# Streamed matmul operands moved by 192 bytes relative to the weight tiles

## Chip, cores and metric

One core of a Trainium2 chip. The metric is the device time of one execution in microseconds; the time before is the median of three runs.

## What is computed

A decoder trunk of four layers on 256 tokens of width 1024, in float32. Each layer adds half a feed-forward block, a mixer, and half a second feed-forward block; a norm ends it. The mixers are gated DeltaNet (layers 0 and 3), stick-breaking attention (layer 1) and a sparse attention with latent keys (layer 2).

```python
for i in range(DEPTH):
    x = x + 0.5 * swiglu(rmsnorm(x, ffn1_norm[i]), ffn1_w_gu[i], ffn1_w_down[i])
    h = rmsnorm(x, mix_norm[i])
    x = x + mixer[i % 3](h)
    x = x + 0.5 * swiglu(rmsnorm(x, ffn2_norm[i]), ffn2_w_gu[i], ffn2_w_down[i])
return rmsnorm(x, final_norm)

def swiglu(h, w_gu, w_down):        # hidden width 2816
    gate, up = jnp.split(h @ w_gu, 2, axis=-1)
    return (jax.nn.silu(gate) * up) @ w_down
```

## The kernel before

All activations lie transposed in SBUF, features on the 128 partitions and tokens along the free axis. A float32 operand of a large product is split into a high part, rounded to the four-byte type float32r, and a low part, the rest; a product is then hi x hi, hi x lo and lo x hi summed in PSUM. All products of this kind run through line 43, `Bank.mm(out, lhsT, rhs)`: `lhsT`, a tile of 128 x 128, is loaded as the stationary operand, and `rhs` is streamed.

Weights arrive in chunks of 1 MB (`chunk`, line 164, three buffers r). A chunk is four pieces of 512 columns; `piece` writes each one's high part h on ScalarE (line 170) and its low part l on VectorE (line 171). h and l have ten buffers each. One stationary operand is 128 columns (512 bytes of each partition) of a piece, so its offset in h or l is a multiple of 512 bytes.

The streamed operands:

- x2, the layer's input times the norm's gain, split: for each of 8 tiles of features 256 columns of the high part and then 256 of the low part (lines 222 and 223). In the profile its name is x, since the program leaves out numbers.
- ah and al, the split hidden activations of the feed-forward block (lines 199 and 200).
- oh and ol, the split heads of a mixer, and lath and latl, the split latents of the sparse attention.

A feed-forward block has 11 steps of 256 hidden columns. A step's gate and up projections (`tile_wide`) are 64 products into bankG: in turn a wide one, h with 512 columns of x2 (high and low part side by side), and a narrow one, l with 256 columns of the high part. Its down projection (`rows`) is 48 products into bankA, each of 256 columns of ah or al. There are 8 blocks, so 2,816 wide and as many narrow products of x2. In the mixers the projections are narrow products of x2 (`tiles2`), and the output projection (`out_proj`) calls `rows` with oh and ol, into bankG. In stick-breaking attention 96 products for the values have h or l as the streamed operand, 512 columns, and x2 as the stationary one. Each mixer has small products besides, in float32 and float16, into bankA.

The order of the products is fixed when the program is made: mixers' side work are generators that `pump` advances between groups of products by a count of estimated time, which no address enters.

Tiles lie in pools, one behind the other in the order const, raw, hi, lo, big, wk; each starts on a multiple of 32 bytes. Sizes and first bytes below are those of the placed program, in bytes of a partition.

| tile | pool | buffers x size | first byte | within 512 |
|---|---|---|---|---|
| h | hi | 10 x 2048 | 57184 | 352 |
| l | lo | 10 x 2048 | 77664 | 352 |
| x2 | big | 1 x 16384 | 98144 | 352 |
| oh, ol, lath, latl and others | big | 8 x 8192 | 114528 | 352 |
| ah | wk | 6 x 1024 | 194592 | 32 |
| al | wk | 6 x 1024 | 200736 | 32 |
| ntri (a table of stick-breaking) | wk | 512 | 211968 | 0 |

The distance of a product is here the first byte of the streamed operand minus that of the weight tile, within 512. It is 0 for x2, oh, ol, lath and latl with h and l (128, 256 or 384 for the products of lath and latl whose weight tiles have 96 columns), and 32 - 352, which is 192, for ah and al. Plain float32 products of two tiles of big, as kT with kT, have distance 0, and u (32) with E (big) has 192. The streamed operand of ntri starts at 320. The last tile of wk ends at byte 228808 of 229376.

Of the kernel before, what the change touches and what calls it, by code (L numbers as in the profile page):

```python
# [11 lines left out]
F32 = mybir.dt.float32  # L12
# [8 lines left out]
P = 128  # L21
T = 256          # tokens
D = 1024
KT = D // P      # k tiles of the model width
F = 2816
NS = F // 256    # steps of a feed-forward block, 256 hidden columns each
# [3 lines left out]
RS = 1024.0      # scale of the residuals kept in float16  # L30

# Everything is kept transposed: [feature on partitions, token].  A float32 matmul operand x is split
# exactly into hi = x rounded to float32r and lo = x - hi; hi*hi + lo*hi + hi*lo in PSUM carries float32.


class Bank:
    """One PSUM bank that several accumulation groups share."""
# [16 lines left out]
    def tr(self, out, x):  # L54
        """Transposes a [128, 128] float32 tile; the only kind of write to its part of the bank."""
        self.nc.tensor.transpose(out, x, self.k.ident)  # L56
        self.k.now += 0.11
# [8 lines left out]
class Trunk:  # L66

    def __init__(self, tc, ctx, a):
        self.tc, self.nc, self.a = tc, tc.nc, a
        nc = self.nc  # L70
        pool = lambda **k: ctx.enter_context(tc.tile_pool(**k))
        self.const = pool(name="const", bufs=1)
        self.raw = pool(name="raw", bufs=3)
        self.hip = pool(name="hi", bufs=10)
        self.lop = pool(name="lo", bufs=10)
        self.big = pool(name="big", bufs=8)
        self.wk = pool(name="wk", bufs=2)
        self.ps = pool(name="ps", bufs=4, space=bass.MemoryType.PSUM)
        self.side, self.now = [], 0.0
        self.act_set("silu_and_others")  # L80
        c = self.const
        self.x = c.tile([P, KT, T], F32, name="x")
        self.gains = c.tile([P, 13, KT], F32, name="gains")
        self.ones = c.tile([P, P], F32, name="ones")
        nc.gpsimd.memset(self.ones, 1.0)
        self.ident = c.tile([P, P], F32, name="ident")
        bf = c.tile([P, 2, P], BF16, name="bf")
        self.identb, self.scap = (bf[:, i] for i in range(2))
        hf = c.tile([P, 3, P], F16, name="hf")
        self.identh, self.identk, self.m1 = (hf[:, i] for i in range(3))  # L90
        self.consts = ((self.ident, a["ident"]), (bf, a["bf"]), (hf, a["hf"]))
        self.pad = c.tile([P, T], F32, name="pad")
        nc.gpsimd.memset(self.pad, 0.0)
        self.pcs = [c.tile([P, 2, 3 + T], F32, name="pc%d" % i) for i in range(2)]
        for pc in self.pcs:
            nc.gpsimd.memset(pc[:, :, :3], 0.0)

    def table(self, name):
        """A mixer's constants, side by side."""
        t = self.wk.tile([P, 1024], F32, name="tab", tag="tab", bufs=1)  # L100
        src = self.a[name]
        self.nc.sync.dma_start(t[:, :src.shape[1]], src)
        return t
# [13 lines left out]
    def bank(self, tag="A"):  # L117
        """A: small products and a feed-forward's sums; G: the big projections."""
        return Bank(self, self.ps.tile([P, 512], F32, name="bank" + tag, tag=tag))

    # ---- interleaving: side work (generators) advances between groups of the big products.  A generator
    # yields how long (us on TensorE's clock, as counted here) its next stage's operands are expected to take,
    # or a condition that its next stage waits for.
# [6 lines left out]
    def pump(self, n=None):  # L130
        """Run up to n ready stages; only the first few (width) generators are under way."""
        for _ in range(n or self.burst):
            g = min(self.side[:self.width], key=self.due, default=None)
            if g is None or self.due(g) > self.now:
                return
            self.step(g)
# [8 lines left out]
    def wait(self, done):  # L145
        """Run side work until done()."""
        while not done():
            g = min(self.side[:self.width], key=self.due)
            assert self.due(g) < math.inf
            self.now = max(self.now, self.due(g))  # L150
            self.step(g)
# [8 lines left out]
    def chunk(self, src, w=2048, pw=512, pool=(), parts=1):  # L160
        """A [128, w] chunk of weights as (hi, lo) pieces of pw columns; the pieces in pool are split by GpSimd."""
# [12 lines left out]
    def first_chunk(self, src, n):  # L174
        """The kernel's start: the first chunk and x arrive in parts and are split as they come."""
# [27 lines left out]
    def rsqrt(self, a, n):  # L203
        """Newton's iteration for a ** -0.5 on a small tile."""
# [20 lines left out]
    def norm_in(self, n):  # L225
        """x times the gain, split; the tokens' factors come later (rstd)."""
# [5 lines left out]
    def spread(self, cols):  # L232
        """[token, 1] columns (SBUF) -> a bank with each as a row on all partitions."""
# [5 lines left out]
    def rstd(self, st):  # L239
        """1 / rms(x) per token, into st: compact [token, 2] and as rows [128, T]."""  # L240
# [28 lines left out]
    # GDN's chunks of the input projection, (kind, head pair): keys 0, values 1, queries 2, gate 3  # L269
    gdn_order = ((0, 0), (0, 1), (0, 2), (3, 0), (0, 3), (3, 1), (2, 0), (1, 0), (1, 1), (1, 2), (1, 3),  # L270
                 (2, 1), (3, 2), (2, 2), (2, 3), (3, 3))
    korder = (0, 2, 4, 6, 1, 3, 5, 7)    # the order in which a block's last products finish x

    def tiles2(self, pieces, xg, order=None):
        """Two M tiles (8 k tiles each) of one chunk into one bank."""
# [8 lines left out]
    def tile_wide(self, pieces, m, order=None):  # L284
        """One M tile into a bank: the columns of hi * hi and those of hi * lo + lo * hi side by side."""
# [9 lines left out]
    def rows(self, acc, pieces, a2, last, done=None):  # L295
        """acc[d, t] += w[f, d] a[f, t] for the chunk's two k tiles."""
# [73 lines left out]
    def gdn(self, i, n):  # L370
# [17 lines left out]
        # b and a: [16, T]  # L388
# [4 lines left out]
        # pairs (head, chunk of tokens) are kept in the order of the projections: head pair, chunk, head of the pair  # L393
# [13 lines left out]
        def gates():  # L407
# [29 lines left out]
            # E[j, i] = exp(G_i - G_j) for i >= j, else 0; eGb: exp(G_i) of the second chunk as rows  # L437
# [13 lines left out]
        def conv2(b, kind, c, dst):  # L451
            """Convolution and silu of two projected heads: dst [128, 2, T]."""
# [3 lines left out]
            # chunks are stored k, v, q; the convolution's channels q, k, v  # L456
# [18 lines left out]
        def keys(c):  # L475
# [23 lines left out]
            # A = I + L (unit lower triangular), transposed, in two float16 parts  # L499
# [8 lines left out]
            # the inverse X of A in float16 by merging blocks; XT its transpose  # L508
# [26 lines left out]
            # float32: with R = I - A X, the inverse is X + X R + X R R (+ X R^3, below float32)  # L535
# [46 lines left out]
        def delta(c):  # L582
# [36 lines left out]
            # the queries' factor s = dk^-0.5 / |q| goes into the output's norm: s * rsqrt(s^2 ss/128 + eps)  # L619
# [53 lines left out]
    def sb(self, n):  # L673
# [31 lines left out]
        def attend(h, qk):  # L705
            # z^T: [keys, queries]; columns: key tile 0 x all queries, key tile 1 x queries of tile 1
# [38 lines left out]
    def rms_factor(self, sq, n, ones, out):  # L745
        """rsqrt(mean of squares + eps) per token from a squared tile, into out [token, 2]."""
# [11 lines left out]
    def dsa(self, n):  # L758
# [15 lines left out]
        # tiles of the input projection: cq 0..2, index key | rotary key 3, ckv 4..5; 6: the normed index key  # L774
# [25 lines left out]
        def weights():  # L800
            """A query's weights of the index heads, times the factor of its latent, which relu lets through."""
# [6 lines left out]
        def latents(c, b):  # L808
            """Evacuate a chunk of the input projection: factor of the token, squares, gain and split."""
# [21 lines left out]
        def index_keys():  # L831
            """kidx[:, e]: the rotated index key in the rows of a tile's head e, zeros in the other's; rotary keys into K."""
# [49 lines left out]
        def select():  # L882
            """The 64 largest of each row are struck out; what is struck out and causal is selected: neg 0, else -1e30."""
# [33 lines left out]
        def attend(h):  # L917
# [21 lines left out]
            for i in range(3):       # (key 0, query 0), (key 0, query 1), (key 1, query 1)  # L939
                bt.tr(bt.t[:, i * P:(i + 1) * P], p[:, i * P:(i + 1) * P])  # L940
# [25 lines left out]
        # the index first, so that the selection runs beside the projections of queries, keys and values  # L966
# [61 lines left out]
    def final(self, out):  # L1028
        """The last norm, beside the last products: to be called with each tile of x as it is done."""
# [53 lines left out]
def cols(w):  # L1083
    """[1024, n * 256] -> [n, 128, 2048]: per chunk two M tiles of 8 k tiles."""
# [4 lines left out]
def rows(w):  # L1089
    """[n * 256, 1024] -> [n, 128, 2048]: per chunk two k tiles."""  # L1090
# [4 lines left out]
def pack_ffn(gu, down):  # L1095
    out = np.empty((gu.shape[0], NS, 3, 128, 2048), gu.dtype)
    for l in range(gu.shape[0]):
        # a chunk: gate tile, up tile
# [6 lines left out]
def feat(g):  # L1105
    """[n * 128] -> [128, n]"""
# [3 lines left out]
def pack(x, ffn1_norm, ffn1_w_gu, ffn1_w_down, mix_norm, ffn2_norm, ffn2_w_gu, ffn2_w_down,  # L1110
# [41 lines left out]
    # constants of the shapes  # L1152
# [10 lines left out]
    for v, s in enumerate((2, 4, 8, 16, 32, 64)):  # L1163
        c = np.arange(64)
        blk = c // s                      # block of 2s of the c-th first-half column
# [41 lines left out]
```

## Time and profile before

| | us |
|---|---|
| median of three runs | 2090.61 |
| lowest and highest | 2089.94, 2092.35 |
| span of the profiled execution | 2092.3 |

The profile gives the profiled execution no time besides its span. Engines in it: PE is TensorE's products, PEld its weight loads, DVE VectorE, ACT ScalarE, POOL GpSimd, SP the queue that issues DMAs. Products are pipelined, and the end of one is modelled, so records of following products overlap, and the pitch from one start to the next is shorter than a record. In the names of a product, as bankG<-x,h, the streamed operand stands ahead of the stationary one.

### The profile page before, as it was taken

To read this page: it belongs to the slowest core of one execution; us is meant where nothing else is said; L and a number is where in the kernel's file an instruction comes from. 1 tells how busy PE (TensorE), PEld (TensorE's weight loads), DVE (VectorE), ACT (ScalarE), POOL (GpSimd) and SP (SyncE) were. 2 spreads that over 40 slices of the span, in tenths; PEclk is the share of its full clock that TensorE was granted. 3 is DMA by queue.
4 is the path that set the end of the run, shared out by engine and by line. 5 is a ranking of instruction groups with operands and counts; after the bars stand their busy time and mean duration, and the time that the engine had idled before them with its cause. 6 is when DMAs were issued, how large, how long until landed. Compare 5 with 4: busy or idle time off the path is not lost.

```text
span 2092.3 us, 38898 instructions
## 1 busy us (share of the span) xinstructions
PE 2037.1 (97%) x14762; PEld 1886.2 (90%) x14762; DVE 1646.0 (79%) x3456; ACT 1308.2 (63%) x2804; POOL 161.9 (8%) x145
## 2 busy tenths in 40 slices
PE   8999899999999999999999998999999998999998
PEld 7999899999999989999989997899989998999997
DVE  7778898877887776777787789877787788988776
ACT  6566776665665566655665664765665667766654
POOL 1001311100100010100010013100010013111000
PEclk9999999999999999999999999999999999999999
DMA  7555333555455554555555542455555553235552
GB/s 256 195 188 182 102 105 123 173 190 187 171 206 188 195 179 140 176 184 197 185 184 199 182 153 76 162 187 196 184 182 199 184 179 106 100 119 182 182 199 84
DMA packets 52603, 353.62 MB, mean 169 GB/s; under 512 B 6976, under 2 KB 7872, under 8 KB 10688
## 3 DMA queue, kind: packets, MB, share of 16 engines
q1 hardware_dynamic: 52128, 350.49, 48.4%
q8 instruction: 116, 1.90, 0.4%
q14 instruction: 71, 0.58, 0.1%
q10 hardware_dynamic: 288, 0.66, 0.1%
HBM read 350.07 MB, written 1.05 MB: 168 GB/s over the span
## 4 chain that ended last, share of the span: by engine, by line
PE 82%; DVE 12%; ACT 4%; issue 1%; POOL 0%; DMA 0%; SPq 0%; ACTq 0%; DVEq 0%; POOLq 0%
PE bankG L43 55%; PE bankA L43 25%; DVE l L171 5%; ACT x L222 1%; DVE kT L466 1%; PE bankA L56 1%; ACT h L170 1%; DVE x L223 1%; DVE rs_t L211 1%; DVE x L302 0%; DVE rs_y L212 0%; DVE rs_t L210 0%; ACT sq L244 0%; DVE vT L466 0%; DVE pc L455 0%
## 5 line engine op out<-in xcount | busy, mean ns | idle before, releaser
L43 PE MATMUL bankG<-x,h 128*128 128x512 f32 (+1 forms) x4192 | 1269.0, 361 | 12.0 <-DVE x L223 12.0
L171 DVE TENSOR_TENSOR l<-r,h 128x512 fp32r<-128x512 f32 x1328 | 936.7, 713 | 374.1 <-ACT h L170 370.9
L170 ACT ACTIVATE h<-r 128x512 fp32r<-128x512 f32 x1328 | 823.0, 627 | 595.5 <-PE bankG L43 337.4
L43 PE MATMUL bankG<-x,l 128*128 128x256 f32 x3504 | 989.2, 282 | 0.0
L43 PEld LDWEIGHTS bankG<-x,h 128*128 128x128 f32 x4192 | 751.3, 189 | 130.1 <-DVE x L223 14.9
L43 PEld LDWEIGHTS bankG<-x,l 128*128 128x128 f32 x3504 | 666.5, 190 | 0.1
L43 PE MATMUL bankA<-ah,l 128*128 128x256 f32 x1408 | 389.2, 276 | 0.0
L43 PE MATMUL bankA<-ah,h 128*128 128x256 f32 x1408 | 389.2, 276 | 0.0
L43 PE MATMUL bankA<-al,h 128*128 128x256 f32 x1408 | 389.1, 276 | 0.0
L43 PEld LDWEIGHTS bankA<-ah,h 128*128 128x128 f32 x1408 | 264.4, 188 | 3.3
L43 PEld LDWEIGHTS bankA<-al,h 128*128 128x128 f32 x1408 | 264.5, 188 | 0.0
L43 PEld LDWEIGHTS bankA<-ah,l 128*128 128x128 f32 x1408 | 264.4, 188 | 0.0
L330 DVE TENSOR_TENSOR e<-e,bankG 128x256 f32<-128x256 f32 x352 | 145.9, 414 | 4.6 <-ACT e L329 4.6
L329 ACT ACTIVATE e<-bankG 128x256 f32<-128x256 f32 x352 | 129.3, 367 | 11.5 <-PE bankG L43 11.5
L245 POOL TENSOR_TENSOR sq<-sq 128x512 f32<-128x512 f32 x12 | 15.5, 1294 | 1473.8 <-ACT sq L244 1473.8
L342 DVE TENSOR_TENSOR e<-e,rb 128x512 f32<-128x512 f32 x176 | 121.0, 691 | 5.3 <-ACT rb L259 0.2
L199 ACT ACTIVATE ah<-e 128x256 fp32r<-128x256 f32 x176 | 72.6, 417 | 21.4 <-DVE e L344 21.3
L343 ACT ACTIVATE e<-e 128x256 f32<-128x256 f32 x176 | 71.3, 405 | 7.2 <-DVE e L342 7.2
L43 PE MATMUL bankG<-oh,h 128*128 128x256 f32 x256 | 74.5, 291 | 0.0
L344 DVE TENSOR_TENSOR e<-e 128x256 f32<-128x256 f32 x176 | 73.8, 419 | 0.7 <-ACT e L343 0.7
L200 DVE TENSOR_TENSOR al<-e,ah 128x256 fp32r<-128x256 f32 x176 | 73.1, 419 | 0.5 <-ACT ah L199 0.5
L43 PE MATMUL bankG<-oh,l 128*128 128x256 f32 x256 | 72.5, 283 | 0.0
(290 smaller groups left out, 1704.7 us busy)
## 6 DMA issues: line engine op xcount, KB each, us to landing
r<-in_ffn SPq DMA_DIRECT2D x262, 1024.0 KB, 4.9
r<-in_gdn_in SPq DMA_DIRECT2D x32, 1024.0 KB, 4.9
r<-in_gdn_out SPq DMA_DIRECT2D x8, 1024.0 KB, 4.9
r<-in_sb_qk SPq DMA_DIRECT2D x8, 1024.0 KB, 4.9
r<-in_sb_v SPq DMA_DIRECT2D x4, 1024.0 KB, 4.9
r<-in_sb_out SPq DMA_DIRECT2D x4, 1024.0 KB, 4.9
r<-in_dsa_out SPq DMA_DIRECT2D x4, 1024.0 KB, 4.9
r<-in_dsa_in SPq DMA_DIRECT2D x3, 1024.0 KB, 4.8
```

The costliest lines, as they stand in the source:

```text
L43: self.nc.tensor.matmul(out, lhsT, rhs, start=self.fresh, stop=stop, skip_group_check=True)
L56: self.nc.tensor.transpose(out, x, self.k.ident)
L170: self.nc.scalar.activation(h[:, :pw], src, AF.Copy)
L171: (self.nc.gpsimd if pool else self.nc.vector).tensor_sub(l[:, :pw], src, h[:, :pw].bitcast(F32))
L199: self.nc.scalar.activation(dh, src, AF.Copy)
L200: self.nc.vector.tensor_sub(dl, src, dh.bitcast(F32))
L211: nc.vector.scalar_tensor_tensor(t, t, -0.5, a, op0=ALU.mult, op1=ALU.mult)
L329: nc.scalar.activation(e[:, m * T:(m + 1) * T], b.t[:, :T], AF.Copy)
L330: nc.vector.tensor_add(e[:, m * T:(m + 1) * T], e[:, m * T:(m + 1) * T], b.t[:, T:])
L342: nc.vector.tensor_mul(e2, e2, st["rb"][:, None, :].to_broadcast([P, 2, T]))
L343: nc.scalar.activation(e[:, :T], e[:, :T], AF.Silu)
L344: nc.vector.tensor_mul(e[:, T:], e[:, T:], e[:, :T])
```

## The change

Two tiles that nothing writes or reads are put around the pool big: one of 48 float32 numbers (192 bytes) ahead of it, one of 80 (320 bytes) behind it. All tiles of big so start 192 bytes later, and all of wk 512 bytes later; const, raw, hi and lo stay. The distance of x2, oh, ol, lath and latl to h and l becomes 192, that of h to x2 in the values of stick-breaking attention 320, and that of ah and al stays 192. Everywhere else the diff only empties comments and docstrings; lines from 77 on have numbers higher by 3.

```diff
         self.raw = pool(name="raw", bufs=3)
         self.hip = pool(name="hi", bufs=10)
         self.lop = pool(name="lo", bufs=10)
+
+        pool(name="gap0", bufs=1).tile([P, 48], F32, name="gap0")
         self.big = pool(name="big", bufs=8)
+        pool(name="gap1", bufs=1).tile([P, 80], F32, name="gap1")
         self.wk = pool(name="wk", bufs=2)
         self.ps = pool(name="ps", bufs=4, space=bass.MemoryType.PSUM)
```

## Rows read from the trace of the kernel before

**Rows 1.** The page: span, busy time of each engine, granted clock by slices

```profile
span 2092.3 us, 38898 instructions
...
PE 2037.1 (97%) x14762; PEld 1886.2 (90%) x14762; DVE 1646.0 (79%) x3456; ACT 1308.2 (63%) x2804; POOL 161.9 (8%) x145
...
PEclk9999999999999999999999999999999999999999
```

**Rows 2.** Stages: stretch, length, busy time (count) of each engine, clock, DMA

```profile
192.80:378.40 185.60, 175.22 (x1670) 169.76 (x1669) 165.97 (x440) 127.18 (x325) 40.43 (x36) 0.98 0.34 117
378.40:562.60 184.20, 183.68 (x1240) 168.31 (x1240) 142.94 (x271) 113.88 (x234) 5.34 (x4) 1.00 0.55 188
...
747.10:858.60 111.50, 109.33 (x785) 103.42 (x784) 71.28 (x141) 71.59 (x133) 5.30 (x4) 0.98 0.46 159
...
1227.60:1339.90 112.30, 101.20 (x724) 91.37 (x723) 95.37 (x269) 66.11 (x149) 29.10 (x25) 0.98 0.32 111
```

**Rows 3.** The chain of waits in a feed-forward block: start, length, what

```profile
41.43 11.10 PE bankG L43 x64
52.53 5.45 PE bankA L43 x48
```

**Rows 4.** TensorE by form, whole run: count, busy us, mean ns, idle

```profile
L43 PE MATMUL bankG<-x,h 128*128 128x512 f32 x2816 | 990.2, 394 | 11.7 <-DVE x L223 11.7
L43 PE MATMUL bankG<-x,l 128*128 128x256 f32 x3504 | 989.2, 282 | 0.0
L43 PE MATMUL bankA<-ah,l 128*128 128x256 f32 x1408 | 389.2, 276 | 0.0
...
L43 PE MATMUL bankA<-al,h 128*128 128x256 f32 x1408 | 389.1, 276 | 0.0
L43 PE MATMUL bankG<-x,h 128*128 128x256 f32 x1376 | 278.9, 292 | 0.2 <-DVE x L223 0.2
...
L43 PE MATMUL bankG<-oh,l 128*128 128x256 f32 x256 | 72.5, 283 | 0.0
L43 PE MATMUL bankG<-ol,h 128*128 128x256 f32 x256 | 72.3, 283 | 0.0
...
L43 PE MATMUL bankG<-lath,l 128*128 128x256 f32 x36 | 10.1, 282 | 0.0
...
L43 PE MATMUL bankA<-u,E 128*128 128x128 f32 x64 | 9.4, 275 | 0.0
...
L43 PE MATMUL bankA<-kT 128*128 128x128 f32 x64 | 8.4, 275 | 0.0
...
L43 PE MATMUL bankG<-lath,l 128*96 128x256 f32 x16 | 5.2, 326 | 0.0
...
L56 PE MATMUL bankA<-ident,on 128*128 128x128 f32 x32 | 4.8, 272 | 0.0
```

**Rows 5.** TensorE by form between 41.4 and 180 us, in the first block

```profile
L43 PE MATMUL bankG<-x,h 128*128 128x512 f32 x275 | 95.8, 391 | 0.0
L43 PE MATMUL bankG<-x,l 128*128 128x256 f32 x274 | 76.7, 280 | 0.0
```

**Rows 6.** The chain in the four mixers: shares by line, and two pieces

```profile
by line: PE bankG L43 32.3%; PE bankA L43 15.9%; DVE l L171 11.8%; DVE kT L466 5.3%; issue 4.1%; PE bankA L56 3.6%; DVE vT L466 1.8%; DVE rs_t L211 1.8%; DVE pc L455 1.7%; DVE qT L466 1.6%; DVE rs_t L210 1.3%; ACT x L222 1.2%; ACT h L170 1.
...
by line: PE bankG L43 70.8%; PE bankA L43 17.2%; DVE l L171 6.7%; issue 1.4%; ACT h L170 1.0%; DVE x L302 0.9%; PE bankA L56 0.6%; DVE rs_y L212 0.5%; DVE rs_t L211 0.4%; DVE rs_t L210 0.3%; DVE rs_y L208 0.1%; DVE ms L254 0.1%; ACTq L170 0
...
802.05 4.31 PE bankG L43 x36
...
by line: PE bankG L43 21.0%; DVE l L171 10.2%; PE bankA L43 8.0%; issue 6.7%; DVE m L893 4.5%; DVE m L876 4.2%; DVE m L891 3.8%; DVE rs_t L211 2.9%; ACT p L932 2.5%; DVE qtmp L910 2.4%; DVE rs_y L212 2.2%; DVE K L997 2.2%; ACT K L998 2.0%; 
...
1325.86 14.15 PE bankG L43 x118
...
by line: PE bankG L43 32.2%; PE bankA L43 15.8%; DVE l L171 11.8%; DVE kT L466 5.3%; issue 4.2%; PE bankA L56 3.3%; DVE vT L466 1.8%; DVE rs_t L211 1.8%; DVE pc L455 1.7%; DVE qT L466 1.6%; DVE rs_t L210 1.3%; ACT x L222 1.2%; ACT h L170 1.
```

**Rows 7.** Timeline of TensorE, values of stick-breaking: first and last of twelve

```profile
768.46 0.39 PE L43 MATMUL bankG<-l,x 128*128 128x512 f32 x1
768.69 0.62 PE L43 MATMUL bankG<-h,x 128*128 128x512 f32 x2
...
775.94 0.39 PE L43 MATMUL bankG<-l,x 128*128 128x512 f32 x1
```

**Rows 8.** Weight loads by form, whole run

```profile
L43 PEld LDWEIGHTS bankA<-ah,l 128*128 128x128 f32 x1408 | 264.4, 188 | 0.0
...
L43 PEld LDWEIGHTS bankG<-oh,l 128*128 128x128 f32 x256 | 49.1, 192 | 0.1
```

**Rows 9.** TensorE's waits, longest in total: us, times, longest

```profile
PE bankA L56 <- DVE rs_y L212: 12.0, 11, 2.2
PE bankG L43 <- DVE x L223: 12.0, 10, 7.5
```

**Rows 10.** VectorE by form in a feed-forward block, 395.9 to 554.7 us

```profile
L171 DVE TENSOR_TENSOR l<-r,h 128x512 fp32r<-128x512 f32 x117 | 80.7, 692 | 38.9 <-ACT h L170 38.7
```

**Rows 11.** TensorE by form in stick-breaking attention: products with ntri

```profile
L43 PE MATMUL bankA<-sl,ntri 128*128 128x384 f32 x8 | 2.7, 340 | 0.0
```

**Rows 12.** Timeline of TensorE, x2 with weights of 16 columns

```profile
197.03 0.39 PE L43 MATMUL bankA<-x,bah 128*16 128x256 f32 x2
...
198.05 0.40 PE L43 MATMUL bankA<-x,bah 128*16 128x256 f32 x2
```

## The prediction

> **What bounds the kernel now.** I read the page first, then the stages, then the chain of waits, then the groups by form. The page has TensorE busy 97% of a span of 2092.3 us, with the granted clock at 0.9 or more in every slice [rows 1]; but a busy TensorE is not a TensorE at its peak, so the stages come next. They are of two kinds. Between the marks 378.4 and 562.6 one feed-forward block takes 184.2 us, with VectorE busy 142.9, ScalarE 113.9 and the clock full; the mixers take 185.6 (gated DeltaNet), 111.5 (stick-breaking) and 112.3 (sparse attention) [rows 2]. In the chain, a step of a feed-forward block is two pieces and nothing else: 64 products into bankG in 11.10 us, then 48 into bankA in 5.45 [rows 3]. Eleven times 16.55 is 182.1 of the 184.2 us. What matters in these blocks is therefore the pitch of the products, the time from one start to the next: 11.10 / 32 = 346.9 ns for a wide and a narrow one together (512 and 256 columns), and 5.45 / 48 = 113.5 ns for each of the narrow ones of the down projection. The groups by form give longer means (276 ns for ah and al) [rows 4], since a record runs to the end of its pipeline: 276 - 113.5 = 162.5, and (391 + 280 - 346.9) / 2 = 162 for the pair [rows 5, 3]. Means less 162.5 are pitches.
>
> **The excess.** At 2.4 GHz 256 columns last 106.7 ns and 512 last 213.3. What each product takes beyond that sorts by the distance of its operands (start of the streamed operand minus start of the weight tile, within 512 bytes):
> - distance 0, narrow, in a mixer: 36 in 4.31 us, 118 in 14.15 [rows 6], so 119.7 and 119.9; excess 13.1.
> - distance 0, wide with h as the moving operand: 33 between the starts 768.46 and 775.94 [rows 7], so 226.7; excess 13.4.
> - distance 0, a wide and a narrow one in turn: 346.9 against 320; excess 26.9 for two, 13.4 each.
> - distance 192 (ah and al): 113.5; excess 6.9.
>
> So at distance 0 every product of split operands pays about 13.4 ns whatever its width, and at 192 one of 256 columns pays 6.9. The cleanest pair is oh against ah: the same function, the same shapes, the same weight tiles, 283 ns against 276 [rows 4]. The weight loads differ too, 192 ns against 188 [rows 8].
>
> **The change, part by part.** It removes and adds no instruction, no wait and no DMA; the two tiles are never written. Order, queues and buffer counts stay. (1) gap0 moves everything in big by 192 bytes. Weight and streamed operand go from distance 0 to 192 for x2, oh, ol, lath and latl, which is the distance of ah and al now. (2) gap1 makes the shift of wk 512 in all, so ah and al keep their distance.
>
> Feed-forward blocks: a pair becomes 320 + 2 x 6.9 = 333.8 ns, the 64 products 10.68 us where they took 11.10. With 8 blocks of 11 steps, 88 x 0.42 = 36.9 us. All of it reaches the end if nothing else is late: VectorE has 142.9 us of work for a block that would take 179.6, ScalarE 113.9, and the waits of TensorE are short, the longest group 12.0 us in the whole run [rows 2, 9]. Were a split late instead, VectorE's weight split would be it, 692 ns each [rows 10]; its load would be 80% of the block, so I add nothing.
>
> Mixers: a narrow product goes from 119.9 to 113.5, 5.3% of its time. Only those on the chain count. bankG holds 32.3% of 185.7 us, 32.2% of 185.6, 70.8% of 111.6 and 21.0% of 112.4 [rows 6]: 60.0 + 59.8 + 79.0 + 23.6 = 222.4 us. Of that, 96 wide ones with h moving (21.8 us) have their distance turned the other way, to 320, which no row of a product with a full weight load shows; from below, they could stay at 226.7, from above pay the 17.8 ns of excess (340 - 162.5 - 160) of the product of 384 columns with ntri, whose distance is 320 [rows 11], 96 x 4.4 = 0.4 us more. I take the same 6.4 ns as for the rest, since 320 is 192 the other way: 0.6 us. The other 200.6 us give 10.7. Bounds: none of the gain where VectorE and ScalarE work is late too (3.6 us, stick-breaking alone), and all 2,988 narrow products times 6.4 (19.1 us; 1,376 and 688 of x, 768 of oh and ol, 156 of lath and latl [rows 4]). I take 11.3, by the chain's share.
>
> Other operands that change their distance: plain float32 products. kT with kT is at 0 and u with E at 192, and both last 275 ns [rows 4]; I count nothing, with 0.3 us either way (some 100 small products, and 3 ns between 275 and the 272 of a transpose).
>
> Sum: 2092.3 - 36.9 - 11.3 = 2044.1 in the profile's terms. The profiled execution's span is 1.7 us above the median of 2090.61, so 2042.4.
>
> **A rule against it.** The Trainium skill's page SBUF — State Buffer, section Who interferes with whom, gives TensorE two independent read ports, one for the moving operand and one for weight loads, and says that it never waits on anyone. By that rule no distance could matter and the time would stay at 2090.6. The rows at 13.4 and 6.9 ns above speak against it as far as one trace can; the rule's outcome is the rival of no change below.
>
> **Rivals.**
> - *The excess at distance 192 grows with width.* 6.9 ns per 256 columns, so 13.8 for a wide product. For it: with one width only at distance 192, the trace can't tell a charge per product from one per column, and the wide rows at 226.7 are twice 113.4. Against: then the wide ones with h moving pay nothing for distance 0, while narrow ones pay 6.4. A pair would take 320 + 20.7 = 340.7, saving 6.2 x 2,816 = 17.5 us; with 10.7 from the mixers, 2092.3 - 28.2 - 1.7 = 2062.4.
> - *Only narrow products gain.* In the stretch of rows 5 the pair splits into 391 - 280 = 111 ns more for the wide one, so 229 and 118. If the 229 stays, a pair takes 342.5, saving 4.4 x 2,816 = 12.4 us, and with 10.7 from the mixers it is 2067.5.
> - *No change.* All narrow products at 120 write to bankG, all at 113.5 to bankA, so the cause could be the bank or the stage. For it: the float32 products above, both in bankA, don't care for the distance. Against: with 16-column weights, x2 at its present place streams at 0.113 (nine products between 197.03 and 198.05 [rows 12]), so x2 alone isn't slow; what is slow is x2 with a full weight load, and oh and ah differ in little but place. Also here: the placement drops the unused tiles. 2090.6.
> - *Slower.* 192 may be good only inside runs of equal products, as in the down projection, and the alternation of 512 and 256 columns may fall each time on the weight load's reads. The nearest row is the 17.8 ns of the product of 384 columns [rows 11]. Place: the gate and up projections. A pair would take 320 + 35.6 = 355.6, 8.7 x 2,816 = 24.5 us more; if narrow ones in the mixers paid it too, 222.4 x 3.8% = 8.5 more: 2123.6. With the mixers' gain kept, it decides from a pair of 350.9 ns on (346.9 + 11.3 / 2.816), or 11.23 us for the 64.
>
> **How the numbers follow.** The likeliest, every product at 6.9 ns: 0.53; its own range is 2034 (all mixer gains) to 2050 (the least). Per-column excess 0.20, narrow ones alone 0.08, still faster than 2034 0.04, no change 0.08, slower 0.07. The range 2034 to 2070 takes in the first three. I call a difference under 0.2% (4 us) the same, about what a measurement of this kernel can tell: faster 0.85, same 0.08, slower 0.07.
>
> **What would show it.** Right: in the chain 10.68 us for the 64 products (10.90 by the per-column rival, 10.96 where only narrow ones gain, 11.10 with no change, over 11.23 if slower), and 5.45 still for the 48. Means by form: 276 for x with l and for oh and ol, 383 for the wide one in a stretch like that of rows 5 (390 by the per-column rival). Mixers: 36 products of x in 4.09 us. Weight loads at 188 for oh. Blocks at 179.6 us, with VectorE's work as before; if a block is longer than its products, VectorE has become late. Wrong first of all would be the step that extends 6.9 ns from 256 columns to 512.

## The result: slower, and the profile after

The changed kernel takes 2115.41 us (median of four runs, 2113.41 to 2116.32) against 2090.36: a ratio of 1.0117, interval 1.0103 to 1.0132. The forecast was 2042.4 with a range from 2034 to 2070. The span is 2114.0 us, 21.7 more than before, with the same 38898 instructions.

The stages tell where it came from. These are the stretches of [rows 2], by the changed kernel's own marks, with the second gated DeltaNet mixer as well (stretch, length, busy time and count of each engine, clock, DMA):

```profile
194.00:377.80 183.80, 171.58 (x1671) 166.13 (x1670) 165.41 (x440) 126.68 (x325) 40.66 (x36) 0.98 0.34 117
377.80:565.90 188.10, 187.56 (x1240) 170.68 (x1239) 143.02 (x271) 113.98 (x234) 5.34 (x4) 1.00 0.53 185
754.00:863.10 109.10, 107.07 (x786) 100.86 (x786) 71.17 (x141) 71.24 (x133) 5.29 (x4) 0.98 0.46 162
1239.40:1351.10 111.70, 100.05 (x724) 90.02 (x723) 95.06 (x270) 65.91 (x149) 27.15 (x25) 0.98 0.32 111
1727.50:1911.50 184.00, 173.35 (x1670) 167.96 (x1669) 165.51 (x440) 126.62 (x324) 41.27 (x36) 0.97 0.34 115
```

The mixers became shorter: 183.8 + 109.1 + 111.7 + 184.0 = 588.6 us, where they had 185.6 + 111.5 + 112.3 + 185.6 = 595.0, so 6.4 less. A feed-forward block became longer, 188.1 where it had 184.2, and the eight of them together 21.7 + 6.4 = 28.1 us. Clock and VectorE's work in the block are as they were. The chain of waits in such a block, which answers to [rows 3], has both pieces longer:

```profile
38.89 11.31 PE bankG L43 x64
50.20 5.65 PE bankA L43 x48
```

A wide and a narrow product now take 11.31 / 32 = 353.4 ns, where 346.9 were measured and 333.8 forecast. And the products of ah and al, whose distance of 192 did not change, take 5.65 / 48 = 117.7 ns where they took 113.5. That is 88 x 0.21 and 88 x 0.20 us, 36 in all; the blocks lost less, 28.1. In part this is since a few of the steps of before already took 5.65 and 11.29 us (below), and in part luck: the 64 products that open the first block took 14.11 us in the profile before and 11.77 here, and in the runs below with the same 64 products it lies anywhere between 11.8 and 13.8.

In the mixers the forecast pitch is there, though not everywhere. The last group of the output projection in the first of them, by form, with 276 where oh and ol had 283 [rows 4], and one piece of the chain in stick-breaking attention, which had 4.31 us in [rows 6] and was forecast at 4.09:

```profile
L43 PE MATMUL bankG<-oh,l 128*128 128x256 f32 x18 | 5.0, 276 | 0.0
```

```profile
808.35 4.10 PE bankG L43 x36
```

Over the whole run, though, the changed kernel has 281 for the three kinds of ah and al, 399 for the wide products of x2 (276 and 394 in [rows 4]), and 279 for oh with l, between the two values:

```profile
L43 PE MATMUL bankG<-x,h 128*128 128x512 f32 x2816 | 1003.0, 399 | 11.6 <-DVE x L226 11.6
...
L43 PE MATMUL bankA<-ah,l 128*128 128x256 f32 x1408 | 395.6, 281 | 0.0
...
L43 PE MATMUL bankG<-oh,l 128*128 128x256 f32 x256 | 71.2, 279 | 0.0
```

So there are two questions: why do wide and narrow products in turn not gain at 192, and why did ah and al, which stayed at 192, become slower?

### The profile page after: what moved, and what is told of

Its sections match the earlier page's. It is cut to its first block, busy times and chain, and to the rows that moved or that the text cites. A ratio compares the mean times of both kernels' runs of the same rounds, so it can differ in the third digit from the quotient of the medians.

```text
span 2114.0 us, 38898 instructions
## 1 busy us (share of the span) xinstructions
PE 2056.7 (97%) x14762; PEld 1894.1 (90%) x14762; DVE 1646.3 (78%) x3456; ACT 1306.7 (62%) x2804; POOL 161.1 (8%) x145
## 4 chain that ended last, share of the span: by engine, by line
PE 84%; DVE 10%; ACT 3%; issue 1%; POOL 0%; DMA 0%; SPq 0%; DVEq 0%; ACTq 0%; POOLq 0%
PE bankG L43 56%; PE bankA L43 27%; DVE l L174 4%; ACT x L225 1%; DVE kT L469 1%; PE bankA L56 1%; DVE x L226 1%; ACT h L173 1%; DVE rs_t L214 0%; DVE rs_y L215 0%; DVE rs_t L213 0%; DVE vT L469 0%; DVE pc L458 0%; DVE qT L469 0%; ACT sq L247 0%
## 5 line engine op out<-in xcount | busy, mean ns | idle before, releaser
L43 PE MATMUL bankG<-x,h 128*128 128x512 f32 (+1 forms) x4192 | 1275.6, 363 | 11.8 <-DVE x L226 11.8
L43 PE MATMUL bankA<-al,h 128*128 128x256 f32 x1408 | 395.7, 281 | 0.0
L43 PE MATMUL bankA<-ah,l 128*128 128x256 f32 x1408 | 395.6, 281 | 0.0
L43 PE MATMUL bankA<-ah,h 128*128 128x256 f32 x1408 | 395.6, 281 | 0.0
L43 PEld LDWEIGHTS bankA<-ah,h 128*128 128x128 f32 x1408 | 270.0, 192 | 3.7
```

What stands on the lines that cost most here:

```text
L43: self.nc.tensor.matmul(out, lhsT, rhs, start=self.fresh, stop=stop, skip_group_check=True)
```

## The experiments

Each run is one edit of the kernel before or of the changed one. For runs without an interval the time is a single one; the kernel before took 2090 to 2092 us beside them. "64" and "48" are the chain's pieces of a feed-forward step.

**Is it where ah lies?** Only wk is moved, by 512 bytes.

```diff
         self.big = pool(name="big", bufs=8)
+        pool(name="gap1", bufs=1).tile([P, 128], F32, name="gap1")
```

> Only wk moves, by 512 bytes; x2, oh and ol stay at distance 0, ah and al at 192. Theory A (the pitch of ah depends on the state in which the gate and up products leave TensorE, not on where ah lies): nothing changes, 48 products of ah in 5.45 us, 64 of x2 in 11.10, span 2092 us. Theory B (512 bytes are not the period, so ah lies worse after the move of wk): 48 products of ah in 5.65 us, 64 of x2 still in 11.10, span 2092 + 88 x 0.20 = 2110 us.

Measured: 2091.0 us, and the chain is that of before.

```profile
55.86 11.10 PE bankG L43 x64
66.96 5.45 PE bankA L43 x48
```

Theory B falls: the new place of wk costs nothing.

**Does ah follow the products ahead of it?** In the changed kernel one small float16 product goes between the gate and up products and the down products of a step.

```diff
             if s > 0:
+                d = self.bank("G")
+                d.mm(d.t[:, :P], self.identh, self.identh)
                 self.rows(acc, self.chunk(w[s - 1, 2]), (acts.pop(0), acts.pop(0)), False)
```

> The changed kernel with one small float16 product (128 columns, its result unused) put between the gate and up products and the down products of a step, from the second step on. Theory A: after the interruption ah starts in another state, and most of its 48 products take 113.5 ns again; less 80 x 0.18 us, plus about 0.12 us for each interruption: 2114 - 14 + 10 = 2110 us, with the gate and up products at 11.31 still. Theory B: ah stays at 117.7 ns; 2114 + 10 = 2124 us.

Measured: 2109.5 us. The timeline of TensorE around one such product:

```profile
69.08 0.23 PE L43 MATMUL bankG<-hf 128*128 128x128 f16 x1
69.12 0.36 PE L43 MATMUL bankA<-ah,h 128*128 128x256 f32 x1
...
69.56 0.28 PE L43 MATMUL bankA<-ah,h 128*128 128x256 f32 x1
...
71.03 0.28 PE L43 MATMUL bankA<-ah,l 128*128 128x256 f32 x1
```

From 69.56 to 71.03 there are 13 products, 0.113 us each, at the same addresses that gave 117.7 ns without the interruption. The pitch of such a row is a state: it depends on how the row begins, and then holds. The 48 with the interruption take 5.50 to 5.51 us. The 64 products behind them still take 11.37 us with the small one, so the pair at 192 gains nothing by the better start.

**Other distances for x2.** x2 gets a tile with 512 bytes to spare, and each of the eight feed-forward blocks uses it at another offset; the tiles behind x2 move by 512. Of the edit this shows the tile alone.

```diff
-    def xg_tiles(self):
-        self.x2 = self.big.tile([P, KT, 2 * T], F32R, name="x2", tag="xg", bufs=1)
+    def xg_tiles(self, off=0):
+        t = self.big.tile([P, KT * 2 * T + 128], F32R, name="x2", tag="xg", bufs=1)
+        self.x2 = t[:, off:off + KT * 2 * T].rearrange("p (j c) -> p j c", j=KT)
```

> The eight feed-forward blocks have x2 at the distances 0, 64, 128, 192, 256, 320, 384 and 448 in this order; x2 in the mixers, oh, ol, lath and latl at 0, ah and al at 192 as before. Theory A: at 0 11.10 and 5.45 us for the 64 and the 48 products, at 192 11.31 and 5.65; ah follows x2's distance in the other blocks too, taking values other than 5.45 although its own distance is the same throughout. Theory B: 48 products of ah take one and the same time, 5.65 us, in all eight blocks. A period of 128 bytes would give the block at 128 the values of the one at 0, and the blocks at 64, 192, 320 and 448 one common value.

Measured: 2111.4 us in all. Pieces of the chain from the blocks at 0, 64, 128, 192, 256, 320, 384 and 448:

```profile
73.05 11.10 PE bankG L43 x64
84.15 5.45 PE bankA L43 x48
...
443.17 11.31 PE bankG L43 x64
454.49 5.65 PE bankA L43 x48
460.14 11.29 PE bankG L43 x64
...
624.58 5.65 PE bankA L43 x48
630.23 11.22 PE bankG L43 x64
...
906.78 5.65 PE bankA L43 x48
912.44 11.31 PE bankG L43 x64
...
1100.18 11.10 PE bankG L43 x64
...
1397.02 11.29 PE bankG L43 x64
1408.30 5.45 PE bankA L43 x48
...
1600.82 11.22 PE bankG L43 x64
...
1974.01 11.31 PE bankG L43 x64
```

The values repeat after 256 bytes, not after 128. Of these distances 0 (and 256) is the best for the kernel's alternation of widths, and ah takes 5.45 or 5.65 behind it without having moved: theory A. At 64 and at 320 the two values take turns from step to step for the whole block: 64 products in 11.31 us and 48 in 5.65, then 64 in 11.29 and 48 in 5.45, then again. The gate and up products thus hand a state on to ah, and which one depends on their distance and on the state that they found. A second scan put the blocks at 32, 96, 160, 224, 16, 48, 8 and 240 and the mixers at 64 and 128.

> The eight feed-forward blocks have x2 at the distances 32, 96, 160, 224, 16, 48, 8 and 240 in this order, the four mixers at 64, 128, 64 and 128; all else as before. The scan before gave 11.10, 11.30, 11.22, 11.31 us for the 64 products at 0, 64, 128, 192 and the same again 256 higher. Theory C (streamed and loaded operand meet in units of 64 bytes, period 256): 8, 16, 32 and 48 give values between or equal to those at 0 and 64, none under 11.10. Rival: the products depend on finer steps, and some distance gives 10.68 to 10.90. In the mixers narrow products in a row took 120 ns at 0 and mostly 113.5 at 192; if one unit of 64 is what counts, 64 gives 113.5 and 128 gives 120; if only 192 is good, 64 gives 117 to 120.

Measured: 2103.0 us. Past its first steps, the 64 took 11.11 us in the block at 32, 11.21 at 96, 11.11 at 160, 11.30 at 224, 11.10 at 16, 11.09 at 48, 11.31 at 8 and 11.27 at 240, with 5.65, 5.46, 5.45, 5.44, 5.46, 5.65, 5.65 and 5.44 behind them. Two of the pieces, at 160 and at 8:

```profile
614.11 11.11 PE bankG L43 x64
...
1577.43 11.30 PE bankG L43 x64
```

The figures that theory C gave for 8 to 48 came out, to 0.01 us. Its units of 64 bytes don't hold even so: 160 is better than both 128 (11.22) and 192 (11.31), and 8 is as bad as 192 while 0 and 16 stand at 11.10. The rival's finer steps are there, but none of the sixteen distances came near 10.90. In the mixers the narrow products of x2 took 118.3 ns at 64 (35 in 4.14 us) and 118.4 at 128 (36 in 4.26), so neither serves them as 192 does.

**Mixers alone.** x2 stays at 0 in the feed-forward blocks and goes to 192 in the mixers, with oh, ol, lath and latl (the tile of x2 as above with 192 bytes to spare, and 320 bytes behind big).

> x2 at distance 0 in the feed-forward blocks and at 192 in the mixers; oh, ol, lath, latl at 192. If the products of the mixers gain by themselves what the changed kernel shows there (185.6 to 183.8, 111.5 to 109.1, 112.3 to 111.7, 185.6 to 184.0 us by the marks of the norms), and the feed-forward blocks keep 11.10 and 5.45: 2090.4 - 6.5 = 2084 us. If the loss is tied to the mixers (the state they leave) or to the move of wk: feed-forward blocks at 188 us, 2110 us or more.

Measured: 2085.53 us, ratio 0.9976 (0.9966 to 0.9986). The mixers' gain is a real one, and the loss lies in the feed-forward blocks alone.

**Narrow products only.** In the changed kernel each wide product is made as two narrow ones.

```diff
-            b.mm(b.t, wh, self.x2[:, j], False)
+            b.mm(b.t[:, :T], wh, self.x2[:, j, :T], False)
+            b.mm(b.t[:, T:], wh, self.x2[:, j, T:], False)
```

> The changed kernel's distances (192), but each wide product of the gate and up projections is made as two narrow ones, so that a step has 96 narrow products where it had 64: same columns, one more weight load in three. Theory A with the loss in the alternation of widths: narrow products in a row at 192 take 113.5 ns as in the mixers, 96 in 10.89 us, and ah follows in the good state, 48 in 5.45: 2115 - 88 x (0.42 + 0.20) = 2060 us, faster than both kernels. If the extra load costs, or the bad state is tied to the feed-forward blocks: 96 products at 117.7 ns, 11.30 us, and 2115 us.

> The kernel before (distance 0) with each wide product as two narrow ones. If distance 0 costs a row of narrow products what it costs in the mixers: 96 x 120 = 11.52 us, and 2090 + 88 x 0.42 = 2127 us. If it is only the count of loads or the stage that matters, the same time as the kernel with three narrow products at 192.

Measured: at 192, 2071.9 us, ratio 0.9920 (0.9898 to 0.9941); at 0, 2120.6 us. The chain at 192, then at 0:

```profile
54.65 10.88 PE bankG L43 x96
65.53 5.44 PE bankA L43 x48
```

```profile
57.59 11.50 PE bankG L43 x96
69.09 5.46 PE bankA L43 x48
```

Narrow products in a row take 10.88 / 96 = 113.3 ns at 192 and 119.8 at 0, as the forecast read from [rows 3] and [rows 6]. Two narrow products at 192 take 226.6 ns together, no more than a wide one in a row of wide ones (below), so the additional weight load costs nothing that shows.

**Is it the alternation or the width?** Both distances again, with the 8 wide products of a tile first and then the 8 narrow ones.

> The changed kernel's distances, with the 16 products of a tile in another order: first the 8 wide ones, then the 8 narrow ones, so that widths alternate twice a tile and not at every product. If the alternation is what 192 doesn't suit (a wide product in a row of wide ones then pays 6.9 ns as a narrow one does): 64 products in 10.68 us and ah 5.45, 2115 - 88 x 0.83 = 2042 us. If the charge is per column: 10.90, 2061 us. If wide products are slow at 192 in any order (226 to 235 ns): 10.9 to 11.3 us, 2060 to 2115 us, with the narrow ones at 113.5 ns by themselves.

> The kernel before (distance 0) with the same other order: first 8 wide, then 8 narrow products of a tile. If every product pays 13.4 ns at 0 whatever stands beside it, nothing changes: 64 products in 11.10 us, 2090 us. If the cost at 0 depends on the neighbours, wide ones in a row take the 226.7 ns of the values of stick-breaking and narrow ones 113 to 120 ns, 10.9 to 11.1 us.

Measured: at 192, 2092.04 us, ratio 1.0009 (0.9999 to 1.0019), the 64 in 11.09; at 0, 2106.5 us, the 64 in 11.16. The timeline of TensorE at 192 has the rows of equal width merged:

```profile
57.96 1.07 PE L43 MATMUL bankG<-x,l 128*128 128x256 f32 x8
58.87 2.02 PE L43 MATMUL bankG<-x,h 128*128 128x512 f32 x8
60.73 1.07 PE L43 MATMUL bankG<-x,l 128*128 128x256 f32 x8
```

Eight narrow ones last from 57.96 to 58.87, 114 ns each; eight wide ones from 58.87 to 60.73, 232.5 each, an excess of 19.2 ns. At distance 0 the wide ones of [rows 7], with h moving, pay 13.4, and those of x2 in this order 16.5 (30 rows of eight between 400 and 545 us, 229.8 ns on average; narrow ones 118.8). One such row is the time from the first to the second of these starts:

```profile
59.09 2.00 PE L43 MATMUL bankG<-x,h 128*128 128x512 f32 x8
60.93 1.11 PE L43 MATMUL bankG<-x,l 128*128 128x256 f32 x8
```

The distance that suits narrow products is the worse one for wide ones. The alternation has its part too: at 192 the 64 fall from 11.31 us to 11.09 without it, and ah is back at 5.44. Neither of the two figures for distance 0, 11.10 and at most 11.1, came out: it is 11.16. The times of both runs hold more than the products, though. TensorE waits longer for the norm's rs_y, 20.5 us in all at 0 and 21.8 at 192 against 12.0 before [rows 9], which is about 1 us a block:

```profile
PE bankA L56 <- DVE rs_y L212: 20.5, 18, 2.2
```

So 2092.04 isn't the price of the order at 192: its steps take 16.53 us where those of before take 16.55.

**Which weight tile counts?** While a product streams against its own weight tile, the next one's is loaded, h and l in turn (loads are busy for 1886 us beside 2037 of products [rows 1]). l is moved against h, so that a product has one distance to its own tile and another to the one being loaded.

```diff
+        pool(name="gap0", bufs=1).tile([P, 48], F32, name="gap0")
         self.lop = pool(name="lo", bufs=10)
         self.big = pool(name="big", bufs=8)
+        pool(name="gap1", bufs=1).tile([P, 80], F32, name="gap1")
```

> l lies 192 bytes further within 512 than h; x2 and big are at 192 from h and at 0 from l; ah at 192 from h and 0 from l. A wide product of x2 has h as its own weight tile while l is loaded for the next one; a narrow one has l as its own while h is loaded. Theory L (what counts is the distance to the tile that is being loaded meanwhile): wide ones see 0 and take 226.7 ns, narrow ones see 192 and take 113.4, 64 products in 10.88 us; of three ah products one sees 0, 48 in about 5.55 us; 2090 - 88 x 0.12 - some 4 us in the mixers = 2075 us. Theory O (the distance to its own tile counts): wide 233 and narrow 120 ns, 64 in 11.30 us, 2090 + 88 x 0.25 = 2112 us.

> The mirror image: x2 at 0 from h and at 192 from l; ah at 192 from h and 384 from l. Theory L: a wide product sees the loading of l at 192 and takes 233 ns, a narrow one that of h at 0 and takes 120; 64 products in 11.30 us, 2090 + 88 x 0.2 = 2108 us or more. Theory O: wide 226.7, narrow 113.4 ns, 64 in 10.88 us, 2075 us.

Measured: 2111.8 us, ratio 1.0104 (1.0087 to 1.0120), with the first; 2107.4 with its mirror image. The chains in this order:

```profile
57.33 11.20 PE bankG L43 x64
68.53 5.65 PE bankA L43 x48
```

```profile
56.25 11.10 PE bankG L43 x64
67.35 5.67 PE bankA L43 x48
```

Neither theory's 10.88 came out, and neither's 11.30: L and O both fall. The times, 2111.8 and 2107.4, lie next to O's 2112 and L's 2108, but by luck: the pieces that were to add up to them are others. Either arrangement put the products of ah, with two distances in one row, at about 118 ns.

**Chance or program?** The kernel with three narrow products at 192 was run again.

> The three narrow products at 192 once more, since its four runs lay 15.6 us apart (2062.8 to 2078.4) where the kernel before lies within 6. If a run falls by chance into the state in which narrow products take 117.7 ns, a slower profile shows some blocks at 11.30 and 5.65 us for 96 and 48 products; if the spread comes from the mixers, the blocks are at 10.88 and 5.44 in it and the mixers longer. The median should again be some 20 us under the kernel before.

Measured: 2086.5 us, ratio 0.9985 (0.9965 to 1.0005), eleven of its twelve runs between 2078 and 2103: the second series did not repeat the first. Its profile (span 2084.5, against 2061.1) shows why. The first two pieces are from one block, the last two from the next:

```profile
519.75 10.88 PE bankG L43 x96
530.63 5.44 PE bankA L43 x48
...
604.86 11.31 PE bankG L43 x96
616.17 5.65 PE bankA L43 x48
```

Three of the eight blocks were slow throughout, 117.8 ns for every product, and five fast throughout. One program at one set of addresses has two states, and a block stays in the one it began in. Three blocks of 11 steps at 0.43 + 0.21 us are 21 us, which is most of the 23.4 between the two spans. The second series ran on another chip than the first, the chip of the two kernels below too. Whether the share of slow blocks differs from chip to chip isn't shown; that both states occur doesn't hang on it, since one run holds both.

**Setting the state.** The same kernel with the small float16 product after the gate and up products of the second and third step of each block, and with it in every step from the second on.

> Three narrow products at 192 as before, and in each feed-forward block one small float16 product after the gate and up products of the second and of the third step. If the state is set by how a row of products begins, and the float16 product sets the good one (as it did for ah in all steps of the run with the break), every block is at 10.88 and 5.44 us from its third step on, and the runs lie close together near 2061 + 16 x 0.12 = 2063 us. If the state falls by chance also after a float16 product, some blocks stay at 11.31 and 5.65, and the runs spread over 2062 to 2095 as without it.

> The same with the small float16 product in every step from the second on, 80 in all. If it sets the good state each time: 10.88 and 5.44 throughout, 2061 + 80 x 0.12 = 2071 us, the runs close together. If chance: as without it, 10 us later.

Measured: 2069.29 us, ratio 0.9890 (0.9875 to 0.9906), runs from 2065.9 to 2069.8; and 2080.24, ratio 0.9948 (0.9936 to 0.9961), runs from 2079.4 to 2081.5. The chain of the first, at the start of the first block:

```profile
39.95 10.95 PE bankG L43 x97
50.90 5.52 PE bankA L43 x48
56.42 10.88 PE bankG L43 x96
```

All eight blocks run at 10.88 and 5.44 from then on, apart from the interruptions, in both kernels, and the runs lie within 4 us. Six blocks of the first had begun at 113 to 114 ns a product by themselves; the fourth and the sixth had not. In the fourth the 36 products ahead of the small one took 117.8 ns each, and the 48 with it and behind it 5.50 us:

```profile
870.15 4.24 PE bankG L43 x36
...
874.58 5.50 PE bankA L43 x48
```

So the state can be set by the program, and the version with two small products in each block is the fastest kernel here that came out alike each time, 1.1% under the kernel before. An interruption costs 0.07 + 0.08 = 0.15 us by this chain, more than the 0.12 expected, which is part of why both kernels came out later than the 2063 and 2071 us expected. No other kind of interruption was tried; behind the mixers' small float32 products rows begin in either state (below).

## Why the prediction was wrong

**What bounds the kernel: right.** In the chain of every run the pieces of the steps follow each other without a gap, and no split became late: a fast block at 10.88 and 5.44 took 182.0 us by the marks for the 179.5 of its eleven steps, where one of before took 184.2 for 182.1.

**The excess, sorted by distance alone: wrong, in two ways.** The step that failed first is the one the forecast named as the weakest, 6.9 ns carried over from narrow products at 192 to wide ones. A wide product at 192 pays 19 ns in a row of wide ones, and with a narrow one in turn the two pay 353.4 - 320 = 33.4, not 13.8. At 0 both widths paid 13.4, and that they agreed there made a charge per product look general; no row had a wide one at 192. The rival that saw it slower had the place right (gate and up projections) and a threshold, 350.9 ns for a pair, that was passed. Its mechanism, the alternation, was one part: the 64 took 11.31 us with it and 11.09 without. The other part, from 11.09 to the forecast's 10.68, stayed with wide products in rows of equal width. (Its price had a slip: 340 - 162.5 - 160 is 17.5 ns, not 17.8, so its 2123.6 should be some 2 us lower, and the 4.4 ns of the values 4.1.)

The second failure is the sentence that ah and al keep 113.5 ns because they keep their distance. They went to 117.7 with neither moved against h and l. A narrow product at 192 has two states, 113.4 and 117.7 ns, and stays in the one in which its row began. This was no term of the sum or of any rival, and it made up about half of the loss: 88 x 0.20 against 88 x 0.21 us. The trace before already had both values, in its chain at the start of a block, which the forecast left out:

```profile
589.88 5.66 PE bankA L43 x48
595.53 11.29 PE bankG L43 x64
606.83 5.45 PE bankA L43 x48
```

The chain of before has 5.65 or 5.66 us for 48 products five times and 11.29 for 64 three times, each time in the first two steps of a block, and 5.45 and 11.10 behind them. So the kernel before, at distance 0, begins some of its blocks in the slow pitch and leaves it after a step or two; the changed one stays in it. The forecast took 5.45 for the value of the distance, where it was one of two.

**The mixers: right in kind, too large.** 6.4 us came of 11.3. Narrow products of x2, oh and ol do run at 113.4, but not all of them, as the mean of 279 for oh with l says: rows that begin again after each small product begin in either state. In the first mixer, rows of 12 products of x2 took 1.42 us at 316.03 and 1.38 at 327.87, 118.3 and 115 ns. The forecast took every narrow product on the chain for a fast one. Its term for the 96 wide products of the values, a gain of 0.6 us, was a loss of 0.2: at 320 they took 228.9 ns (27 between the starts 776.95 and 783.13) where they had taken 226.7.

**The rival of no change** rested in part on the Trainium skill's two independent read ports (SBUF — State Buffer, Who interferes with whom). With nothing but addresses moved, narrow products in a row went from 119.8 to 113.3 ns, so the rule doesn't cover this case. The rival's other argument, the bank, is gone with it: x2 and oh ran at 113.4 into bankG.

**What stays open** is the mechanism itself: why 256 bytes are the period, why width and distance act together, and why neither the own weight tile nor the one being loaded decides alone. What the runs show is that addresses change the pitches that occur, and that a small product at the start of a row can choose between them; why the rows of before leave the slow pitch, those of the scan's blocks at 64 and 320 change it at every step and those of the changed kernel keep it isn't settled. One clue is in the traces of both kernels: at a granted clock of 0.50, the 1.2 GHz level, three wide products of the values took 1.28 us before (from 765.53 to 766.81, at distance 0) and 1.28 after (from 772.62 to 773.90, at 320). That is 426.7 ns each, their 512 columns at 1.2 GHz: at this level there was no excess.

## What to carry to other kernels

Where a kernel is bound by a steady row of products, read the pitch from the chain in every stage and look for two values at the same addresses before you put a value down to an address. A layout found good for one width or order of products is to be measured again for another. And a time that sits in one of two states by chance can be made to sit in the better one: here two tiny products a block took 17 us off the narrow products at 192 (2086.5 to 2069.3), while the layout by itself lost 25.

## What the runs showed of the hardware

- Rows of products of 256 float32r columns held one of several steady pitches for a whole block: 113.3, 117.7 or 119.8 ns, where 106.7 would be the columns alone at 2.4 GHz, the level of the granted clock of 1.00 in these blocks.
- At 192 the first two were both seen in one program in one run (10.88 and 11.31 us for 96).
- One float16 product of 128 columns put the row behind it into the 113.3 ns state in every block, 16 and 80 times a run, also where the row ahead of it ran at 117.8.
- Moving the streamed operand against the weights changed the pitch with a period of 256 bytes: 11.10, 11.31 and 11.29 in turn, 11.22 and 11.31 us for 64 products at 0, 64, 128 and 192, and the same at 256, 320, 384 and 448.
- In rows of eight, products of 512 columns took 229.8 ns at 0 and 232.5 at 192, where products of 256 columns took 118.8 and 114.
